# A hybrid SSD and attention step: norm weight by broadcast, first gate product ahead, y's banks emptied first, scan entry behind a piece

## The chip, the cores and the metric

The kernel runs on one core of a Trainium2 chip. The metric is the device time of one execution in microseconds (us). The engines are TensorE (PE in the profile; PEld is its weight load), VectorE (DVE), ScalarE (ACT), GpSimd (POOL) and SyncE (SP), which here issues the DMAs. Each engine works through its own instructions in order and waits on semaphores for the others.

## What is computed

Two layers on a residual stream of 1,024 prompt tokens and 64 sample tokens (8 requests of 8 tokens) with 1,024 features: a Mamba-2 SSD layer, then a latent-attention layer, then a last norm. All is float32 to the outside. This change concerns the SSD layer alone:

```python
u    = rms_norm(h, norm_w)                       # x * rsqrt(mean x^2 + eps) * norm_w
proj = u @ w_in                                  # z (2048) | x, B, C (4096) | dt (32)
xbc  = silu(causal_conv(xbc, w, b))              # four taps
y    = ssd_scan(xs, softplus(dt + dt_bias), -exp(a_log), B, C, state)   # chunks of 128
y    = (y + d_skip * xs) * silu(z)
y    = y * rsqrt(mean over each of 8 groups of 256 of y^2 + eps) * ssd_norm_w
h    = h + y @ w_out
```

In a chunk, cb = C B^T is masked and multiplied by a decay matrix M; that times x*dt gives the part within the chunk (py), x*dt faded to the chunk's end times B gives the state's gain (st), and C times the state before gives the rest of y.

## The kernel before

**Precision.** A float32 operand is split into a rounded high part and the rest (xh and xl, woh and wol, yha and yla): ACT casts the high part, DVE subtracts it. A product is three matmuls (high*high, high*low, low*high). Line 130 is any such cast, line 131 any such subtraction, lines 89 and 101 the matmuls.

**Order.** For the SSD layer the instructions of every engine stand in the order in which the program emits them, so moving a call in the code moves its instructions on every queue that it uses. Tokens go in 9 tiles (8 of 128, the last with the 64 sample tokens).

**PSUM banks** have tags: tr 2 (all transposes), pj 2 (projections), cb, y, pv and st one each. A tile that takes a bank waits until the last reader of the bank's previous tile is done.

**Start (`First.begin`, `First.norm`).** SP loads x of tile 0, the gate's weights (four quarters z0 to z3, two DMAs each), the norm's weight as one row, the bias of dt sent to all partitions (dtb), and further tiles of x. Four matmuls of a column of ones by the weight's row (two in the program, line 586, each two on the chip) spread it over the partitions into two banks; DVE copies them to the tile nw. Then for each tile: `square` (ACT, with the sum), `root` (DVE, then POOL's power), `scale` (DVE, line 616: x times root times nw, in place), `turn` (8 transposes, line 625), `take` (the split into xh and xl, ACT then DVE), `gate` (24 matmuls with z's weights into pz). The gate's weights are split by `split_z` on ACT and DVE. In between come two batches of small transposes: vecp (convolution weights and norm weights, in the bank of cb) and cvp (the sample's conv state, in the bank of y).

**Groups and scan entry.** Eight groups follow, each with projections of x, B, C and z in pieces (`proj(t)`), the convolution, the silu and a scan over the 9 tiles. Each group's scan runs beside the next group's projections, one step per tile. The first scan is entered at the end of `First`'s projection: front(0) is on TensorE the transposes trp and the product cb of chunk 0; then ACT's last silu; front1(0) reads trp and cb on ACT and DVE, DVE's last step there being cbm, the masked cb.

**Out-projection (`OutProj`, loop over t from 0).** Its first half, "a", runs beside the scan of the last group. Tile i of y is loaded, scaled (ACT, line 1121), transposed into the two tr banks (ytpa, line 1131) and split into yha and yla (lines 130, 131). Tile 0 is multiplied in four parts, in steps 1 to 4, while the weights still arrive: in each step two of the eight weight pieces are scaled and split (woh on ACT, line 1223; wol on DVE, line 1230). The later tiles take a step for each half (`proj`). `scan.ew(t)` is the scan's work off TensorE (M's exponential and product, the state S, y, xD), then front(t+1); `scan.pe(t)` is st and py. In a step the order was: the later tiles' product, scan.ew, the weights, oa.ew (store, split, scale, loads), scan.pe, a part of tile 0, evictions, and the next transposes. yla is the last reader of the tr banks, from which the scan's next transposes (trp, line 809) take theirs.

Of the kernel before, what the change touches and what calls it, by code (L numbers as in the profile page):

```python
# [9 lines left out]
F32 = mybir.dt.float32  # L10
F32R = mybir.dt.float32r
AF = mybir.ActivationFunctionType
# [5 lines left out]
D = 1024  # L18
# [3 lines left out]
T = SEQ + NB * NT  # L22
# [60 lines left out]
PB = dict(PB1)  # L83
# [90 lines left out]
def load_vectors(k, vp, psum):  # L174
# [9 lines left out]
    k.vec = cp.tile([128, 196], F32, name="vec")  # L184
    p = psum.tile([128, 512], F32, tag="cb", name="vecp", bufs=PB["cb"])
    nc.tensor.transpose(p[:, :128], r1, k.ident)
# [370 lines left out]
class First(Flow):  # L557
# [5 lines left out]
    def begin(self):  # L563
        k, nc, cp = self.k, self.k.nc, self.k.cp
        self.load_x(0)
        for q in range(4):
            self.load_z(q)
        row = self.rp.tile([128, RAW], F32, tag="raw", name="nrow", bufs=2)[0:1, :D]
        nc.sync.dma_start(row, k.I["norm_w"][0:1])
        nc.sync.dma_start(k.dtb, k.I["ssd_dt_bias"][0].partition_broadcast(128))  # L570
        for i in range(1, 4):
            self.load_x(i)
        ones = self.xp.tile([1, 128], F32, name="nones")
        nc.gpsimd.memset(ones, 1.0)
        self.ssq = cp.tile([128, 9], F32, name="ssq9")
        nc.gpsimd.memset(self.ssq, 1.0)
        self.rs = cp.tile([128, 9], F32, name="rs9")
        k.dtr = self.zd.tile([128, 9, H], F32, name="dtr")
        nc.gpsimd.memset(k.dtr[64:, 8], 0.0)
        self.square(0)  # L580
        self.root(0)
        self.nw = self.xp.tile([128, D], F32, name="nw")
        for hf in range(2):
            c = slice(512 * hf, 512 * hf + 512)
            p = self.psum.tile([128, 512], F32, tag=("y", "pv")[hf], name=f"nwp{hf}", bufs=1)
            nc.tensor.matmul(p, ones, row[:, c], start=True, stop=True)
            nc.vector.tensor_copy(self.nw[:, c], p)
        self.scale(0)
        self.turn(0)
# [28 lines left out]
    def turn(self, i):  # L618
        m, x = TILES[i][1], self.xt[i]
        self.p[i] = []  # L620
        for q in range(2):
            p = self.psum.tile([128, 512], F32, tag="tr", name=f"xtp{i}_{q}", bufs=PB["tr"])
            for a in range(4):
                d = 4 * q + a
                self.k.nc.tensor.transpose(p[:, a * 128 : a * 128 + m], x[:m, d * 128 : d * 128 + 128], self.k.ident[:m, :m])
            self.p[i].append(p)
# [27 lines left out]
    def norm(self, vectors, states):  # L654
        self.begin()
        self.split_z(0)
        self.split_z(1)
        self.take(0)
        self.split_z(2)
        self.split_z(3)  # L660
        for i in (1, 2):
            self.square(i)
            self.root(i)
        self.scale(1)
        self.turn(1)
        for n in range(1, 10):
            ev = self.gate(n - 1)
            if n < 9:
                self.take(n)
            if n + 2 < 9:  # L670
                self.square(n + 2)
                self.root(n + 2)
            if n + 1 < 9:
                self.scale(n + 1)
            if n + 3 < 9:
                self.load_x(n + 3)
            if n == 2:
                ssd_consts(self.k)
            if n in (2, 6):
                next(vectors)  # L680
            if n in (3, 7):
                next(states)
            if n in (5, 6):
                self.load(n - 5)
            if n in (8, 9):
                self.split(n - 8)
                self.load(n - 6)
            if n + 1 < 9:
                self.turn(n + 1)
            ev()  # L690
# [23 lines left out]
    def blocks(self, dt, nxt, scan_of):  # L714
# [43 lines left out]
        self.conv(3, slice(512, n))  # L758
        self.tails(3)
        scan.front(0)  # L760
        self.silu(1, slice(512, SEQ))
        scan.front1(0)
        return scan

# [333 lines left out]
class OutProj:  # L1098
# [85 lines left out]
    def ew(self, t):  # L1184
        for d, f in ((-1, self.split), (-3, self.scale), (-1, self.load_x), (-5, self.load_y)):
            for i, T in enumerate(self.start):
                if t == T + d and not (i == 0 and self.tag == "a" and d < 0):
                    f(i)
        for i, T in enumerate(self.start):
            if t == T + (4 if i == 0 else 2):  # L1190
                self.store(i)

    def pe(self, t):
# [50 lines left out]
def ssd_groups(k, first, scan, nxt, pools, sp, psum, st, left, right, als):  # L1244
    tc, nc = k.tc, k.nc
    pscan = None
    for g in range(1, G):
        fl, nxt = nxt, Flow(k, g + 1, pools) if g < G - 1 else None
        nscan = Scan(k, fl, (sp, psum))
        for t in range(21):  # L1250
            ev = fl.proj(t)
            fl.weights_in(t)
            if nxt and t == 20:
# [42 lines left out]
    for t in range(B0 + 22):  # L1296
        evs = oa.work(t) if t >= A0 + 4 else []
        if t < 22:
            scan.ew(t)
        if t == 0:  # L1300
            pscan.ew(21)
            oa.split(0)
            oa.load_x(0)
# [29 lines left out]
        if t == 22:  # L1333
            group_rstd(k, 4, 8)
        oa.ew(t)
        ob.ew(t)
# [7 lines left out]
        if t < 21:  # L1344
            scan.pe(t)
        if A0 <= t < A0 + 4:
            evs += oa.work(t)
        for ev in evs:
# [1143 lines left out]
```

## Time and profile before

| | |
|---|---|
| median of 3 runs | 1977.34 us (1976.92 to 1978.05) |
| profiled execution | 1978.51 us, its span 1976.7 us |
| mean granted TensorE clock | 0.985 |
| busy: TensorE, DVE, ACT, POOL | 1890.7, 1185.7, 1108.4, 835.6 us |
| DMA | 206.50 MB, 104 GB/s on the mean |

A row of a timeline has the start in us from the span's start, the time it took, the engine, the line, the operation with output and inputs, and how many it sums up; brackets hold the engine's idle time before it and what ended that. SPq is the issue of a DMA, not its transfer. In the waits view a row has what waited, for what, the us in total, the times and the longest. TensorE's matmuls overlap: their spacing is shorter than their duration.

### The profile page before, as it was taken

The numbers are of one execution on the slowest core, as the hardware profiler recorded it, in microseconds if no ns is written. First come the engines' busy times: TensorE is split into PE (matmuls) and PEld (weight loads), VectorE is DVE, ScalarE is ACT, GpSimd is POOL, SyncE is SP. The second block draws the span as 40 slices with busy tenths as digits, with TensorE's granted clock in tenths as the row PEclk, the third lists the DMA queues.
The fourth block names the chain that finished last, engine by engine and source line by source line (L and its number), as shares of the span: only waits on it lengthen the run. The fifth ranks groups of instructions, "written<-read, shape, count | busy, mean of one in ns | idle before, by whom it ended". The sixth has DMA issues, their size and how long they took to land.

```text
span 1976.7 us, 33806 instructions
## 1 busy us (share of the span) xinstructions
PE 1890.7 (96%) x11957; PEld 1733.9 (88%) x11957; DVE 1185.7 (60%) x2564; ACT 1108.4 (56%) x2604; POOL 835.6 (42%) x1139
## 2 busy tenths in 40 slices
PE   6999999999999999799999999999999999789998
PEld 5999999999999999687687998898888887678887
DVE  5457575757575757545425315476787786666665
ACT  4556666666666666643324314335777777655552
POOL 2137373737373657233000001103565556866661
PEclk9999999999999999899999999999999999899999
DMA  4213332323333332544454432232221213554441
GB/s 140 53 55 90 89 95 84 96 84 95 90 91 92 89 90 85 194 158 155 169 184 141 140 146 82 67 109 68 53 67 40 53 42 97 158 162 143 147 149 38
DMA packets 182403, 206.50 MB, mean 104 GB/s; under 512 B 18989, under 2 KB 147897, under 8 KB 181850
## 3 DMA queue, kind: packets, MB, share of 16 engines
q1 hardware_dynamic: 177402, 185.33, 30.9%
q0 software_dynamic: 4752, 18.88, 2.9%
q8 instruction: 95, 1.56, 0.3%
q14 instruction: 74, 0.61, 0.1%
q10 hardware_dynamic: 80, 0.13, 0.0%
HBM read 150.98 MB, written 53.15 MB: 103 GB/s over the span
## 4 chain that ended last, share of the span: by engine, by line
PE 78%; POOL 7%; issue 4%; DVE 4%; DMA 4%; ACT 3%; SPq 0%; POOLq 0%; DVEq 0%; ACTq 0%
PE pj L89 24%; PE pj L101 9%; PE pq L101 6%; PE pob L101 4%; PE poa L101 4%; POOL kvl L2139 4%; PE py L865 3%; PE sc L1793 2%; PE st L1826 1%; PE o L1859 1%; PE st L1827 1%; PE pz L101 1%; PE st L1828 1%; PE o L1858 1%; PE o L1857 1%
## 5 line engine op out<-in xcount | busy, mean ns | idle before, releaser
L89 PE MATMUL pj<-xh,wih 128*128 128x384 f32 (+1 forms) x768 | 255.1, 332 | 0.0
L89 PE MATMUL pj<-xh,wil 128*128 128x384 f32 (+1 forms) x768 | 250.7, 326 | 0.0
L89 PE MATMUL pj<-xl,wih 128*128 128x384 f32 (+1 forms) x768 | 250.4, 326 | 0.0
L1840 POOL TENSOR_TENSOR tl<-P,th 128x384 fp32r<-128x384 f32 (+1 forms) x144 | 133.0, 929 | 134.0 <-ACT P L1838 74.5
L131 DVE TENSOR_TENSOR wil<-wraw,wih 128x512 fp32r<-128x512 f32 x92 | 70.4, 765 | 172.6 <-ACT wih L130 172.5
L902 POOL TENSOR_TENSOR y<-y,xD 128x256 f32<-128x256 f32 x64 | 84.0, 1313 | 151.4 <-DVE y L901 141.0
L89 PEld LDWEIGHTS pj<-xh,wih 128*128 128x128 f32 x768 | 144.5, 188 | 0.2
L89 PEld LDWEIGHTS pj<-xl,wih 128*128 128x128 f32 x768 | 144.4, 188 | 0.3
L89 PEld LDWEIGHTS pj<-xh,wil 128*128 128x128 f32 x768 | 144.1, 188 | 0.0
L101 PE MATMUL pj<-wih,xh 128*128 128x256 f32 x504 | 143.3, 288 | 0.0
L101 PE MATMUL pj<-wil,xh 128*128 128x256 f32 (+1 forms) x504 | 139.2, 282 | 0.0
L1837 ACT ACTIVATE th<-st 128x512 fp32r<-128x512 f32 x192 | 94.4, 492 | 68.6 <-PE st L1833 46.8
L497 DVE SCALAR_TENSOR_TENSOR acc<-raw,vec,acc 128x1112 f32<-128x1112 f32 x84 | 130.5, 1554 | 0.2
L101 PE MATMUL pj<-wih,xl 128*128 128x256 f32 x448 | 126.6, 283 | 0.0
L2139 POOL TENSOR_TENSOR kvl<-pgr,kvh 128x256 fp32r<-128x256 f32 x128 | 98.2, 794 | 52.4 <-ACT kvh L2137 52.4
L131 POOL TENSOR_TENSOR xddl<-xdd,xddh 128x256 fp32r<-128x256 f32 x64 | 64.0, 1000 | 110.1 <-ACT xddh L130 110.1
L130 ACT CAST Ch<-acc 128x128 fp32r<-128x128 f32 x56 | 16.9, 302 | 157.0 <-PE py L89 157.0
L101 PEld LDWEIGHTS pj<-wih,xh 128*128 128x128 f32 x504 | 96.0, 191 | 0.0
L1838 ACT ACTIVATE P<-st 128x512 f32<-128x512 f32 x192 | 93.4, 486 | 2.7 <-DVE tl L1840 2.0
L101 PEld LDWEIGHTS pj<-wil,xh 128*128 128x128 f32 (+1 forms) x504 | 93.0, 185 | 0.6
L840 ACT ACTIVATE M<-M,tok 128x128 f32<-128x128 f32 (+1 forms) x288 | 90.6, 388 | 1.8 <-DMA M<-acs_d 1.8
L101 PEld LDWEIGHTS pj<-wih,xl 128*128 128x128 f32 x448 | 85.4, 191 | 0.0
(984 smaller groups left out, 6276.7 us busy)
## 6 DMA issues: line engine op xcount, KB each, us to landing
wraw<-in_ssd_w_in SPq DMA_DIRECT2D x92, 256.0 KB
M<-acs_d SPq DMA_DIRECT2D x64, 256.0 KB
y_d<-xD SPq DMA_DIRECT2D x64, 128.0 KB
s<-in_state_ssm SPq DMA_DIRECT2D x32, 256.0 KB
out_s_ssm<-s SPq DMA_DIRECT2D x32, 256.0 KB
wraw<-in_ssd_w_out SPq DMA_DIRECT2D x16, 512.0 KB
q_d<-qt SPq DMA_DIRECT2D x32, 192.0 KB
qp<-q_d SPq DMA_DIRECT2D x8, 768.0 KB
```

The costliest lines, as they stand in the source:

```text
L89: nc.tensor.matmul(out, a, b, start=(i == 0), stop=(i == n - 1))
L101: nc.tensor.matmul(o, a, b, start=(j == 0), stop=(j == len(ops) - 1))
L131: (eng or nc.vector).tensor_tensor(lo, src, hi.bitcast(F32), op=ALU.subtract)
L497: nc.vector.scalar_tensor_tensor(acc, self.raw[bi][:, j : j + n], k.convw[j][:, blk : blk + 1], acc, op0=ALU.mult, op1=ALU.add)
L840: nc.scalar.activation(M[:m, h, :m], M[:m, h, :m], AF.Relu, bias=c.tk[:, 0, 4 * g + h : 4 * g + h + 1], scale=-1.0)
L865: nc.tensor.matmul(py[:m, h * 64 : h * 64 + 64], c.M[:m, h, :m], c.xdt[:m, h * 64 : h * 64 + 64], start=True, stop=True)
L902: nc.gpsimd.tensor_tensor(y[:m], y[:m], c.xD[:m], op=ALU.add)
L1793: nc.tensor.matmul(ps[:, :n], qh[:96, 128 * i : 128 * i + 128], kh[:96, 512 * c : 512 * c + n], start=True, stop=True)
L1837: nc.scalar.activation(th[:, :n], ps[:, :n], AF.Exp, scale=SCALE)
L1838: nc.scalar.activation(P[:, :n], ps[:, :n], AF.Exp, scale=SCALE)
L1840: eng.tensor_tensor(tl[:, :n], P[:, :n], th[:, :n].bitcast(F32), op=ALU.subtract)
L2139: nc.gpsimd.tensor_tensor(rl[:, r], raw[:, r], rh[:, r].bitcast(F32), op=ALU.subtract)
```

## The change

It does four things.

1. **Norm weight.** The row, the ones, the matmuls and the copies go; SP loads the weight into all 128 partitions by one DMA (512 KB), right behind x0. The order of the loads behind it is z0, z1, x1, z2, z3, dtb, x2, x3, x4. An activation of a 128x9 tile without use stands ahead of the first square on ACT.
2. **First tiles.** TensorE's order becomes turn(0), gate(0), turn(1), turn(2), gate(1), turn(3) and so on; odd tiles turn in the banks of cb and st. The square of tile 1 goes ahead of the splits of z2 and z3. Tiles are scaled and turned one step earlier than their gate asked for before. vecp uses the bank of y.
3. **Scan entry.** front(0), the silu and front1(0) are emitted behind proj(0) of the next group.
4. **Out-projection.** The split of y ("cast") goes ahead of the scan's work in each step, and the parts of tile 0 are emitted ahead of scan.pe.

On TensorE at the start, before (nwp is the spread weight, xtp the transposes of a tile, pz the gate's product):

```order
L586 MATMUL nwp_142<-nrow,nones 128x512
L586 MATMUL nwp_145<-nrow,nones 128x512
L625 MATMUL xtp_0_149<-ident,xt_107 128x128 x4
L625 MATMUL xtp_1_154<-ident,xt_107 128x128 x4
L625 MATMUL xtp_0_188<-ident,xt_124 128x128 x4
L625 MATMUL xtp_1_193<-ident,xt_124 128x128 x4
L101 MATMUL pz_199<-zdh_159,xh 128x288
L101 MATMUL pz_199<-zdl_160,xh 128x288
```

and with the change, first

```order
L622 MATMUL xtp_0_143<-ident,xt_107 128x128 x4
L622 MATMUL xtp_1_148<-ident,xt_107 128x128 x4
L101 MATMUL pz_183<-zdh_153,xh 128x288
L101 MATMUL pz_183<-zdl_154,xh 128x288
L101 MATMUL pz_183<-zdh_153,xl 128x288
```

and behind the gate's 24 matmuls

```order
L101 MATMUL pz_183<-zdl_174,xh 128x288
L101 MATMUL pz_183<-zdh_173,xl 128x288
L622 MATMUL xtp_0_208<-ident,xt_117 128x128 x4
L622 MATMUL xtp_1_213<-ident,xt_117 128x128 x4
L622 MATMUL xtp_0_227<-ident,xt_126 128x128 x4
L622 MATMUL xtp_1_232<-ident,xt_126 128x128 x4
L101 MATMUL pz_241<-zdh_153,xh 128x288
```

The spreading is gone, and the second tile's transposes stand behind the first gate's product, with those of the third tile directly behind them.

On TensorE at the scan entry, before (pj_11 is the first group's last piece, pj_0 the next group's first):

```order
L89 MATMUL pj_11_1088<-xh,wil 128x320
L809 MATMUL trp_0_1125<-ident,acc_1012 128x128
L810 MATMUL trp_0_1125<-ident,acc_1012 128x128
L812 MATMUL trp_0_1125<-ident,acc_760 128x128
L814 MATMUL cb_0_1129<-acc_760 128x128
L89 MATMUL pj_0_1149<-xh,wih 128x384
```

and with the change

```order
L89 MATMUL pj_0_1117<-xh,wil 128x384
L809 MATMUL trp_0_1144<-ident,acc_1004 128x128
L810 MATMUL trp_0_1144<-ident,acc_1004 128x128
L812 MATMUL trp_0_1144<-ident,acc_752 128x128
L814 MATMUL cb_0_1148<-acc_752 128x128
L809 MATMUL trp_1_1183<-ident,acc_1004 128x128
L810 MATMUL trp_1_1183<-ident,acc_1004 128x128
L812 MATMUL trp_1_1183<-ident,acc_752 128x128
L814 MATMUL cb_1_1187<-acc_752 128x128
L89 MATMUL pj_1_1189<-xh,wih 128x384
```

The transposes and cb of chunk 0 have moved behind pj_0, directly ahead of those of chunk 1, which stood there before too.

On ACT in the third step of the out-projection, before (y_0 is the scan's first output, M its decay matrix, xddh the faded input's high part, Sh the state's):

```order
L910 ACTIVATE y_0_10765,yssq<-xD_0_10715 128x256
L1223 ACTIVATE woh_10826<-wraw,vec 128x1024
L1223 ACTIVATE woh_10829<-wraw,vec 128x1024
L846 ACTIVATE M_2_10752<-M_2_10752 128x512
L130 CAST xddh_2_10872<-xdd_2_10809 128x256
L130 CAST Sh_1_10877<-S_2_10799 128x256
L130 CAST yha_10887<-ytpa_10858 128x512
L130 CAST yha_10887<-ytpa_10863 128x512
L1121 ACTIVATE yta_10779<-yta_10779,yssq 128x256 x4
```

and with the change

```order
L910 ACTIVATE y_0_10769,yssq<-xD_0_10721 128x256
L1228 ACTIVATE woh_10830<-wraw,vec 128x1024
L1228 ACTIVATE woh_10833<-wraw,vec 128x1024
L130 CAST yha_10872<-ytpa_10850 128x512
L130 CAST yha_10872<-ytpa_10855 128x512
L846 ACTIVATE M_2_10756<-M_2_10756 128x512
L130 CAST xddh_2_10882<-xdd_2_10813 128x256
L130 CAST Sh_1_10887<-S_2_10803 128x256
L1121 ACTIVATE yta_10783<-yta_10783,yssq 128x256 x4
```

The two casts of y have moved from behind the scan's M, xddh and Sh to ahead of them; DVE's yla moves likewise.

On TensorE in the first step of the out-projection with a part, before (poa is tile 0's product):

```order
L809 MATMUL trp_1_10688<-ident,acc_9836 128x128
L810 MATMUL trp_1_10688<-ident,acc_9836 128x128
L812 MATMUL trp_1_10688<-ident,acc_9429 128x128
L814 MATMUL cb_1_10692<-acc_9429 128x128
L89 MATMUL st_0_10729<-xddh_0_10654,BTh_0_10607 128x256
L89 MATMUL st_0_10729<-xddl_0_10655,BTh_0_10607 128x256
L89 MATMUL st_0_10729<-xddh_0_10654,BTl_0_10608 128x256
L865 MATMUL py_0_10730<-xdt_0_10610,M_0_10446 128x64 x4
L1156 MATMUL poa_10738<-woh_10674,yha_10666 128x512
```

and with the change

```order
L809 MATMUL trp_1_10680<-ident,acc_9828 128x128
L810 MATMUL trp_1_10680<-ident,acc_9828 128x128
L812 MATMUL trp_1_10680<-ident,acc_9421 128x128
L814 MATMUL cb_1_10684<-acc_9421 128x128
L1156 MATMUL poa_10686<-woh_10666,yha_10642 128x512
```

The part's first matmul now follows cb_1 directly; its twelve matmuls stand ahead of st_0 and py_0.

The diff:

```diff
--- before.py
+++ after.py
@@ -182,7 +182,7 @@
     nc.sync.dma_start(r2[64:68], I["mla_q_norm_w"].rearrange("o (b c) -> (o b) c", c=128))
     yield
     k.vec = cp.tile([128, 196], F32, name="vec")
-    p = psum.tile([128, 512], F32, tag="cb", name="vecp", bufs=PB["cb"])
+    p = psum.tile([128, 512], F32, tag="y", name="vecp", bufs=PB["y"])
     nc.tensor.transpose(p[:, :128], r1, k.ident)
     nc.tensor.transpose(p[:, 128:196], r2, k.ident[:68, :68])
     nc.vector.tensor_copy(k.vec, p[:, :196])
@@ -563,28 +563,24 @@
     def begin(self):
         k, nc, cp = self.k, self.k.nc, self.k.cp
         self.load_x(0)
-        for q in range(4):
-            self.load_z(q)
-        row = self.rp.tile([128, RAW], F32, tag="raw", name="nrow", bufs=2)[0:1, :D]
-        nc.sync.dma_start(row, k.I["norm_w"][0:1])
+        self.nw = self.xp.tile([128, D], F32, name="nw")
+        nc.sync.dma_start(self.nw, k.I["norm_w"][0].partition_broadcast(128))
+        self.load_z(0)
+        self.load_z(1)
+        self.load_x(1)
+        self.load_z(2)
+        self.load_z(3)
         nc.sync.dma_start(k.dtb, k.I["ssd_dt_bias"][0].partition_broadcast(128))
-        for i in range(1, 4):
+        for i in (2, 3, 4):
             self.load_x(i)
-        ones = self.xp.tile([1, 128], F32, name="nones")
-        nc.gpsimd.memset(ones, 1.0)
         self.ssq = cp.tile([128, 9], F32, name="ssq9")
         nc.gpsimd.memset(self.ssq, 1.0)
         self.rs = cp.tile([128, 9], F32, name="rs9")
         k.dtr = self.zd.tile([128, 9, H], F32, name="dtr")
         nc.gpsimd.memset(k.dtr[64:, 8], 0.0)
+        nc.scalar.activation(self.rs, self.ssq, AF.Square)
         self.square(0)
         self.root(0)
-        self.nw = self.xp.tile([128, D], F32, name="nw")
-        for hf in range(2):
-            c = slice(512 * hf, 512 * hf + 512)
-            p = self.psum.tile([128, 512], F32, tag=("y", "pv")[hf], name=f"nwp{hf}", bufs=1)
-            nc.tensor.matmul(p, ones, row[:, c], start=True, stop=True)
-            nc.vector.tensor_copy(self.nw[:, c], p)
         self.scale(0)
         self.turn(0)
 
@@ -619,7 +615,8 @@
         m, x = TILES[i][1], self.xt[i]
         self.p[i] = []
         for q in range(2):
-            p = self.psum.tile([128, 512], F32, tag="tr", name=f"xtp{i}_{q}", bufs=PB["tr"])
+            tag = ("cb", "st")[q] if i % 2 else "tr"
+            p = self.psum.tile([128, 512], F32, tag=tag, name=f"xtp{i}_{q}", bufs=PB[tag])
             for a in range(4):
                 d = 4 * q + a
                 self.k.nc.tensor.transpose(p[:, a * 128 : a * 128 + m], x[:m, d * 128 : d * 128 + 128], self.k.ident[:m, :m])
@@ -656,37 +653,38 @@
         self.split_z(0)
         self.split_z(1)
         self.take(0)
+        self.square(1)
+        self.root(1)
         self.split_z(2)
         self.split_z(3)
-        for i in (1, 2):
-            self.square(i)
-            self.root(i)
         self.scale(1)
-        self.turn(1)
-        for n in range(1, 10):
-            ev = self.gate(n - 1)
-            if n < 9:
-                self.take(n)
+        self.square(2)
+        self.root(2)
+        for n in range(9):
+            ev = self.gate(n)
+            if n == 0:
+                self.turn(1)
+            if n < 8:
+                self.take(n + 1)
+            if n + 3 < 9:
+                self.square(n + 3)
+                self.root(n + 3)
             if n + 2 < 9:
-                self.square(n + 2)
-                self.root(n + 2)
-            if n + 1 < 9:
-                self.scale(n + 1)
-            if n + 3 < 9:
-                self.load_x(n + 3)
-            if n == 2:
+                self.scale(n + 2)
+                self.turn(n + 2)
+            if n + 5 < 9:
+                self.load_x(n + 5)
+            if n == 1:
                 ssd_consts(self.k)
+            if n in (1, 6):
+                next(vectors)
             if n in (2, 6):
-                next(vectors)
-            if n in (3, 7):
                 next(states)
-            if n in (5, 6):
+            if n in (4, 5):
+                self.load(n - 4)
+            if n in (7, 8):
+                self.split(n - 7)
                 self.load(n - 5)
-            if n in (8, 9):
-                self.split(n - 8)
-                self.load(n - 6)
-            if n + 1 < 9:
-                self.turn(n + 1)
             ev()
 
     def conv(self, bi, c):
@@ -757,10 +755,12 @@
         self.conv0(3, slice(512, n))
         self.conv(3, slice(512, n))
         self.tails(3)
+        return scan
+
+    def enter(self, scan):
         scan.front(0)
         self.silu(1, slice(512, SEQ))
         scan.front1(0)
-        return scan
 
     def state_out(self, t, scan):
         k, nc = self.k, self.k.nc
@@ -1182,13 +1182,18 @@
         k.nc.sync.dma_start(k.h_d[t0 : t0 + m], self.xr[i][:m])
 
     def ew(self, t):
-        for d, f in ((-1, self.split), (-3, self.scale), (-1, self.load_x), (-5, self.load_y)):
+        for d, f in ((-3, self.scale), (-1, self.load_x), (-5, self.load_y)):
             for i, T in enumerate(self.start):
-                if t == T + d and not (i == 0 and self.tag == "a" and d < 0):
+                if t == T + d and not (i == 0 and self.tag == "a"):
                     f(i)
         for i, T in enumerate(self.start):
             if t == T + (4 if i == 0 else 2):
                 self.store(i)
+
+    def cast(self, t):
+        for i, T in enumerate(self.start):
+            if t == T - 1 and i in range(self.tag == "a", 9):
+                self.split(i)
 
     def pe(self, t):
         for i, T in enumerate(self.start):
@@ -1249,6 +1254,8 @@
         nscan = Scan(k, fl, (sp, psum))
         for t in range(21):
             ev = fl.proj(t)
+            if g == 1 and t == 0:
+                first.enter(scan)
             fl.weights_in(t)
             if nxt and t == 20:
                 nxt.split(1)
@@ -1294,12 +1301,14 @@
     oa.yp = st.enter_context(open_pool(tc, name="ya", bufs=1))
     ob = OutProj(k, oa.yp, [], psum, NWA, h_loader(k), "b", B0)
     for t in range(B0 + 22):
-        evs = oa.work(t) if t >= A0 + 4 else []
+        evs = oa.work(t)
+        if t == 0:
+            oa.split(0)
+        oa.cast(t)
         if t < 22:
             scan.ew(t)
         if t == 0:
             pscan.ew(21)
-            oa.split(0)
             oa.load_x(0)
         if t < 4:
             oa.ws += wo.split(wa, 2 * t, 2 * t + 1)
@@ -1332,6 +1341,7 @@
             group_rstd(k, 4, t // 2 - 2)
         if t == 22:
             group_rstd(k, 4, 8)
+        ob.cast(t)
         oa.ew(t)
         ob.ew(t)
         if t == B0 + 13:
@@ -1343,8 +1353,6 @@
             evs += ob.work(t)
         if t < 21:
             scan.pe(t)
-        if A0 <= t < A0 + 4:
-            evs += oa.work(t)
         for ev in evs:
             ev()
         oa.pe(t)
```

## The prediction

> **What bounds the kernel now.** I read the page's busy shares first, then the waits of TensorE, which add up every stall with what ended it.
>
> ```profile
> PE 1890.7 (96%) x11957; PEld 1733.9 (88%) x11957; DVE 1185.7 (60%) x2564; ACT 1108.4 (56%) x2604; POOL 835.6 (42%) x1139
> PE trp L809 <- DVE yla L131: 16.5, 4, 6.8
> PE nwp L586 <- DMA nrow<-in_norm_w: 9.3, 1, 9.3
> PE xtp L625 <- DVE xt L616: 7.6, 2, 5.4
> PE cb L814 <- DVE cbm L833: 1.4, 1, 1.4
> PE trp L809 <- ACT acc L710: 1.4, 1, 1.4
> ```
>
> TensorE is busy for 1890.7 of 1976.7 us, so a gain can only come from its 86 idle us or from time at a lower clock. The last five rows (waited for, us in total, times, longest) are the stalls that this change touches: 9.3 + 7.6 at the start, 16.5 at the banks of y's transposes, 1.4 + 1.4 at the scan entry, together 36.2 us. That is the ceiling. The sum depends on what stands behind each wait, so I read the timeline of each place.
>
> **The start.**
>
> ```profile
> 4.93 1.28 ACT L608 ACT_TABLE_LOAD   x1 [4.93 <-DMA xt<-in_x_prompt]
> 6.17 0.37 SPq L570 DMA_DIRECT2D dtb<-in_ssd_dt_bias  x1
> 6.22 1.06 ACT L608 ACTIVATE sq<-xt 128x1024 f32<-128x1024 f32 x1
> 7.71 0.56 POOL L204 TENSOR_TENSOR rs<-rs,nhalf 128x1 f32<-128x1 f32 x1 [6.51 <-DVE rs L199]
> 9.26 3.75 PE L586 MATMUL nwp<-nrow,nones 1*128 1x512 f32 x4 [9.26 <-DMA nrow<-in_norm_w]
> 13.84 1.28 DVE L616 SCALAR_TENSOR_TENSOR xt<-xt,rs,nw 128x1024 f32<-128x1024 f32 x1
> 15.18 1.97 PE L625 MATMUL xtp<-ident,xt 128*128 128x128 f32 x8 [2.17 <-DVE xt L616]
> 16.33 0.59 ACT L130 CAST xh<-xtp 128x512 fp32r<-128x512 f32 x1 [7.83 <-PE xtp L625]
> 17.67 1.25 ACT L130 CAST zdh<-zraw 128x576 fp32r<-128x576 f32 x2
> 18.41 1.42 DVE L131 TENSOR_TENSOR zdl<-zraw,zdh 128x576 fp32r<-128x576 f32 x2
> 28.26 1.04 PE L625 MATMUL xtp<-ident,xt 128*128 128x128 f32 x8
> 28.26:54.00 25.74, 25.45 (x197) 24.58 (x196) 17.15 (x30) 13.92 (x28) 7.77 (x6) 1.00 0.15 33
> ```
>
> The last row is the windows view (stretch, its length, then busy us of PE, PEld, DVE, ACT and POOL, granted clock, DMA share and GB/s). From the third tile's transposes at 28.26 on, TensorE is full. So the start is worth what it moves that instruction. Eight transposes take 1.97 us at 15.18 and 1.04 there: TensorE ran at half speed before.
>
> Now: x0 lands at 4.93, but the table load comes after it. The dummy activation puts the load ahead, so the square runs 4.93 to 6.0, and the root ends near 7.0 (before, POOL's power ended 1.0 us behind the square's 7.28). The weight now comes as 512 KB instead of 4 KB plus four matmuls (3.75) and two copies. No row of before is this load. The nearest is the decay load M, also one DRAM row sent to all partitions:
>
> ```profile
> 121.79 0.44 SPq L795 DMA_DIRECT2D M<-acs_d  x1
> 125.52 0.69 ACT L840 ACTIVATE M<-M,tok 128x128 f32<-128x128 f32 x2 [1.19 <-DMA M<-acs_d]
> GB/s 0 0 54 160 252 295 339 305 319 345 318 276 76 35 53 64 291 379 410 410 429 422 416 429 416 313 90 41 13 11 15 49 67 57 54 139 391 385 252 233
> ```
>
> M's 256 KB took at most 3.73 us from issue to use; twice that from an issue near 1.6 lands at 9.1, the upper bound. The lower bound is the rate of the strip (40 slices of 0.65 us up to 26): 512 KB at about 320 GB/s, 1.6 us behind x0's landing, 6.5. I take 7.0, since a queue that is already streaming pays M's fixed part only once. Then scale(0) runs 7.05 to 8.3, turn(0) 8.4 to 10.4, xh and xl until 11.7; sq(1) is moved ahead of the last two z splits (11.0 to 12.2; x1, some 2.2 MB into the queue, is there by about 9), the z casts (1.25) follow to 13.4, and scale(1) stands behind their low halves (to 14.2) on DVE, 14.3 to 15.5. The first gate product fills TensorE from 10.2, waiting at the end for the last low half. turn(1) runs from 15.6, xh(1) and sq(3) to 18.9, then root, scale(2) 19.1 to 20.4, turn(2) at 20.5 instead of 28.26: **7.7 us** earlier.
>
> Taken off: slices 12 to 15 of the strip (76, 35, 53 and 64 GB/s, 7.8 to 10.4 us) are the bias load dtb, 16 KB in small pieces, with x1 behind it. x1 is now moved past it, x2 and x3 still stand behind it; 0.4 us for that, between 0 and 3. TensorE idles from about 17 to 20.5, so it may again start at half speed; 1.7 us (one clock window, priced below), between 0 and 3.4. The weight vectors' transpose goes to the bank of y, where the conv state's transposes follow in the same bank and wait for DVE's copy:
>
> ```profile
> 50.01 0.36 DVE L188 COPY vec<-vecp 128x196 f32<-128x196 f32 x1 [0.29 <-PE vecp L187]
> ```
>
> That is 0.36 us plus two hand-overs, 0.6. **Start: 7.7 − 0.4 − 1.7 − 0.6 = +5.0**, from 0.7 to 7.1.
>
> **The scan entry.**
>
> ```profile
> 113.08 0.33 PE L809 MATMUL trp<-ident,acc 128*128 128x128 f32 x1 [1.43 <-ACT acc L710]
> 117.06 1.06 ACT L710 ACTIVATE acc<-acc 128x1024 f32<-128x1024 f32 x1 [2.67 <-DVE acc L696]
> 119.46 0.28 DVE L833 TENSOR_TENSOR cbm<-cb,masku 128x128 f32<-128x128 f32 x1
> 119.79 0.49 PE L814 MATMUL cb<-acc 128*128 128x128 f32 x2 [1.44 <-DVE cbm L833]
> 111.42:114.83 3.41, 1.99 (x14) 1.75 (x13) 0.93 (x2) 2.32 (x4) 0.33 (x2) 1.00 0.00 1
> 892.99:896.42 3.43, 1.07 (x8) 0.74 (x7) 3.34 (x7) 3.21 (x8) 3.02 (x4) 1.00 0.98 334
> 896.42:899.83 3.41, 3.41 (x12) 2.82 (x11) 2.13 (x6) 1.03 (x3) 1.76 (x3) 0.50 0.85 280
> ```
>
> The next group's first piece moves ahead of the chunk's transposes, which takes the first stall away. But the second, at 119.79, is set by ACT's silu at 117.06 and DVE behind it, whose order is unchanged. TensorE reaches it earlier and waits longer: 1.43 + 1.44 become one gap of 2.9. No gain, and a risk: windows with 1.99 of 3.41 us busy kept the clock at 1.00, while one with 1.07 busy (the 2.36 us gap below) was followed by a window at 0.50, which costs half of 3.41, **1.7 us**. A gap of 2.9 leaves some window under half busy unless a window's edge halves it; I take three quarters of the price, **−1.3**, between 0 and −1.7.
>
> The Trainium skill (TensorE: Matmul & The Clock Gate, Part 1) says that the clock falls after an idle window of about 3.4 us and advises against gaps above about 3 us; by it the merged gap would cost nothing and the sum would be 1.3 better. The 0.50 behind a gap of 2.36 disagrees, so the sum goes by the row.
>
> **The first steps of the out-projection.**
>
> ```profile
> 808.41 0.47 PE L809 MATMUL trp<-ident,acc 128*128 128x128 f32 x1 [6.75 <-DVE yla L131]
> 809.20 2.48 DVE L1230 SCALAR_TENSOR_TENSOR wol<-wraw,vec,woh 128x1024 fp32r<-128x1024 f32 x2 [0.25 <-ACT woh L1223]
> 818.56 2.58 DVE L1230 SCALAR_TENSOR_TENSOR wol<-wraw,vec,woh 128x1024 fp32r<-128x1024 f32 x2 [1.20 <-ACT woh L1223]
> 825.16 2.48 DVE L1230 SCALAR_TENSOR_TENSOR wol<-wraw,vec,woh 128x1024 fp32r<-128x1024 f32 x2 [2.28 <-ACT woh L1223]
> 831.06 0.47 PE L809 MATMUL trp<-ident,acc 128*128 128x128 f32 x1 [6.53 <-DVE yla L131]
> 834.99 0.69 DVE L1175 TENSOR_TENSOR xra<-xra,poa 128x512 f32<-128x512 f32 x1 [3.38 <-PE poa L1156]
> 836.25 0.39 PE L101 MATMUL poa<-woh,yha 128*128 128x512 f32 x1
> ```
>
> Here the largest stalls stand, 6.75 and 6.53. The first cast now leaves ahead of the scan's work, so the transposes of 808.41 can start near 804. But the four weight pieces (rows wol) are still split two per step behind the same ACT and DVE work, and each part of tile 0, now ahead of the scan's products, waits for them: wol 0 and 1 end at 811.7 whatever TensorE does. So part 0 ends near 815.2, the scan's st/py behind it near 817.2, part 1 near 820.2; part 2 waits for wol5 (818.56 + 2.58 = 821.1) and ends at 823.5, st/py at 825.1 instead of 820.8. Behind that ACT's cast of Ch (one buffer, free when py has read it) goes later, and with it the last two weight pieces: 828.1 to 830.7 instead of 825.16 to 827.64. y's cast then follows them at once and ends at 832. The first eviction follows DVE's scan work near 834.7, and the whole product of tile 1 starts near 835.4 instead of 836.25. **+0.5** of the 0.85, between −3 (two half-speed windows more) and +6 (half of the stalls go).
>
> **The later steps.**
>
> ```profile
> 878.65 0.33 PE L809 MATMUL trp<-ident,acc 128*128 128x128 f32 x1 [0.86 <-DVE yla L131]
> 894.93 1.27 DVE L131 TENSOR_TENSOR yla<-ytpa,yha 128x512 fp32r<-128x512 f32 x2
> 895.67 0.33 PE L809 MATMUL trp<-ident,acc 128*128 128x128 f32 x1 [2.36 <-DVE yla L131]
> 908.46 0.63 PE L1131 MATMUL ytpa<-ident,yta 128*128 128x128 f32 x4 [1.60 <-ACT xddh L130]
> ```
>
> Nothing but the order on ACT and DVE delays yla there; with y's casts first both stalls go, 0.86 + 2.36, and the half-speed window behind the second, 1.7. M's product and the scan's state come later by the casts' time, which the matmuls of the tile's product cover; without that cover each such step would lose the 1.27 us of yla. At 908.46 the transposes' second half now takes a bank that the cast of the first must free, about 1.9 instead of 1.60: −0.3. **+4.6**, from 2.5 to 4.9. All stages behind are unchanged and shift along.
>
> **Sum:** 5.0 − 1.3 + 0.5 + 4.6 = 8.8 us off the profiled execution's 1978.51, 1969.7; that execution stands 1.2 above the median of 1977.34, so **1968.5** in the median.
>
> **Rivals.** *The stalls really go:* no window is lost at the start (+7.1) or the entry (0), the first steps give half of their stalls (+6), and the later steps 4.6: 17.7, about 1959.6. The size of the 16.5 us row speaks for it, the rows of wol against it. *Gains eaten:* start at its low end (+0.7), entry −1.7, first steps −3, later steps 4.6: +0.6, about 1976.7. For it: each new gap can call up a half-speed window, and DMA-bound tiles at the start. *Slower:* the broadcast load moves at dtb's rate. 16 KB in about 2.6 us is 6.3 GB/s, and 512 KB would take 83 us; scale(0) would run near 85 instead of 13.84, less the 3.8 of the other terms: about 2045. It loses as soon as the weight lands after some 17.6 us (13.84 plus those 3.8). M's row, 256 KB in at most 3.73 us, speaks against it. *The change does not do what it says* is in the forecast already for the entry: the wait there is only merged.
>
> **How the numbers follow.** The forecast 0.57 (its own range 1964 to 1972.5, the terms' nearer bounds), the stalls go 0.18, eaten 0.20, slower 0.05. The range 1960.5 to 1976 reaches into the second and third cases. 0.2%, about what can be told from no change, is 4 us: faster is all of the first two and a quarter of the third, 0.80; same 0.14; slower 0.06, the fourth and the worst edge of the third.
>
> **What would show it.** Right: nw landed by 7 to 9, third tile's transposes near 20 to 22; one gap near 2.9 ahead of the entry's second cb; in the first steps matmuls of poa that wait for wol instead of trp for yla; no trp of later steps that waits for yla. Wrong: the table load not ahead of x0, transposes past 25, an entry without a gap, or the product of tile 1 over 3 us from where it was.

## The result, and the profile after

The changed kernel takes 1968.19 us in the median of 5 runs (1965.63 to 1970.02); the kernel before, on the same chip, 1978.05 (1976.92 to 1980.03). The ratio is 0.9948, with a 95% interval of 0.9933 to 0.9962: 10.3 us faster, between 7.5 and 13.3. The forecast was 8.8 us and 1968.5. The profiled execution has a span of 1966.8 us, 9.9 less than before.

TensorE's waits after the change (what waited, for what, us in total, times, longest):

```profile
PE xtp L622 <- DVE xt L612: 8.5, 1, 8.5
PE poa L1156 <- ACT woh L1228: 6.3, 2, 4.3
PE xtp L622 <- DVE dtr L646: 3.4, 1, 3.4
PE cb L814 <- DVE cbm L833: 3.1, 1, 3.1
PE trp L809 <- DVE yla L131: 2.2, 1, 2.2
PE ytpa L1131 <- DVE yla L131: 1.8, 1, 1.8
PE poa L1156 <- DVE wol L1235: 1.4, 2, 0.8
PE ytpa L1131 <- DVE yha L131: 0.9, 1, 0.9
PE cvp L314 <- DVE vec L188: 0.5, 1, 0.5
```

The row of 16.5 us (trp for yla) is down to 2.2, but more than half of what it lost stands in new rows: the parts of tile 0 wait 6.3 + 1.4 us for the split weights, which they had not shown before. At the scan entry 1.4 + 1.4 has become 3.1. The sums of the waits fell less than the old rows suggest.

Where the time went shows in how far ahead of the kernel before the same instruction stands. The starts are rows of the two timelines:

| place | before | after | ahead | gained since |
|---|---|---|---|---|
| third tile's transposes | 28.26 | 19.99 | 8.27 | 8.27 |
| fourth tile's transposes | 32.56 | 26.79 | 5.77 | −2.50 |
| second cb at the scan entry | 119.79 | 114.83 | 4.96 | −0.81 |
| first transposes of y | 800.02 | 796.63 | 3.39 | −1.57 |
| first whole product (tile 1) | 836.25 | 830.47 | 5.78 | +2.39 |
| tile 6's transposes of y | 906.23 | 895.10 | 11.13 | +5.35 |
| first transposes of half "b" | 948.6 | 938.6 | 10.0 | −1.1 |
| end of the span | 1976.7 | 1966.8 | 9.9 | −0.1 |

The start's own timeline after the change:

```profile
2.01 0.21 ACT L581 ACTIVATE rs<-ssq 128x9 f32<-128x9 f32 x1
5.05 1.06 ACT L604 ACTIVATE sq<-xt 128x1024 f32<-128x1024 f32 x1 [2.83 <-DMA xt<-in_x_prompt]
6.62 0.56 POOL L204 TENSOR_TENSOR rs<-rs,nhalf 128x1 f32<-128x1 f32 x1 [5.54 <-DVE rs L199]
7.21 1.28 DVE L612 SCALAR_TENSOR_TENSOR xt<-xt,rs,nw 128x1024 f32<-128x1024 f32 x1 [0.74 <-POOL rs L204]
8.54 1.97 PE L622 MATMUL xtp<-ident,xt 128*128 128x128 f32 x8 [8.54 <-DVE xt L612]
15.29 1.06 ACT L604 ACTIVATE sq<-xt 128x1024 f32<-128x1024 f32 x1 [1.97 <-DMA xt<-in_x_prompt]
19.99 1.94 PE L622 MATMUL xtp<-ident,xt 128*128 128x128 f32 x8 [3.43 <-DVE dtr L646]
26.79 1.04 PE L622 MATMUL xtp<-ident,xt 128*128 128x128 f32 x8
```

The first scale waits for POOL's root and not for a DMA, so the broadcast weight was there by 7.2: the slow-broadcast rival is out. The third tile's transposes take 1.94 us, half speed, and the fourth tile's come 6.80 behind them instead of the 4.30 of before: 2.50 of the 8.27 us are paid back there. The windows view (columns as in the prediction) shows the granted clock at half in between:

```profile
20.00:23.00 3.00, 3.00 (x14) 3.00 (x15) 1.11 (x2) 1.62 (x3) 0.24 (x1) 0.50 0.14 32
23.00:26.00 3.00, 3.00 (x15) 3.00 (x15) 1.64 (x3) 0.60 (x2) 1.64 (x2) 0.51 0.59 199
```

The out-projection's first steps after the change:

```profile
800.45 0.33 PE L809 MATMUL trp<-ident,acc 128*128 128x128 f32 x1 [2.19 <-DVE yla L131]
805.82 0.80 PE L1156 MATMUL poa<-woh,yha 128*128 128x512 f32 x1 [4.28 <-ACT woh L1228]
807.14 0.80 PE L1156 MATMUL poa<-wol,yha 128*128 128x512 f32 x1 [0.53 <-DVE wol L1235]
823.87 0.49 PE L1156 MATMUL poa<-woh,yha 128*128 128x512 f32 x1 [2.01 <-ACT woh L1228]
825.19 0.80 PE L1156 MATMUL poa<-wol,yha 128*128 128x512 f32 x1 [0.82 <-DVE wol L1235]
830.47 0.47 PE L101 MATMUL poa<-woh,yha 128*128 128x512 f32 x1 [0.62 <-DVE xra L1175]
```

The transposes wait 2.19 us instead of 6.75, and the second stall of 6.53 is gone; but TensorE then waits 4.28 and 2.01 for woh, and 0.53 and 0.82 for wol. So of the 13.3 us (6.75 and 6.53) 11.1 went and 7.6 came back in another place, and the stretch gained only 2.4.

### The profile page after: what moved, and what is told of

It reads as the page before. It is cut to its first block, busy times and chain, and to the rows that moved or that the text cites. A ratio compares the mean times of both kernels' runs of the same rounds, so it can differ in the third digit from the quotient of the medians.

```text
span 1966.8 us, 33784 instructions
## 1 busy us (share of the span) xinstructions
PE 1890.8 (96%) x11953; PEld 1735.2 (88%) x11953; DVE 1185.9 (60%) x2562; ACT 1108.1 (56%) x2605; POOL 833.7 (42%) x1138
## 4 chain that ended last, share of the span: by engine, by line
PE 77%; POOL 7%; issue 4%; DMA 4%; DVE 4%; ACT 3%; SPq 1%; POOLq 0%; DVEq 0%; ACTq 0%
PE pj L89 23%; PE pj L101 9%; PE pq L101 6%; PE pob L101 4%; PE poa L101 4%; POOL kvl L2147 3%; PE py L865 3%; PE sc L1801 2%; PE st L1834 2%; PE st L1835 2%; PE st L1836 2%; PE o L1867 2%; PE o L1866 1%; PE o L1865 1%; PE pk L101 1%
```

## Experiments

Each kernel was compared with runs of the kernel before on the same chip. All intervals are 95%, and gains in us are worked out from the ratios. A statement about a place in the kernel rests on one profiled execution of each kernel.

### The parts alone: e1 to e4

> The kernel before with the start of the change alone (weight by broadcast load, tables first, first gate product ahead, vecp in the bank of y). Theory: the start is worth what it moved in the changed kernel, third tile's transposes near 20.0, then about 5.8 us ahead of before once one half-speed window has been paid, 5.0 to 5.8 behind the wait for vec's copy; in all 5.0 to 5.8 us faster, and nothing else moves. Rival: an earlier start only shifts the wait to the scan entry (its chain runs on ACT and DVE), then under 3 us of it arrive behind the entry.

```diff
-        for q in range(4):
-            self.load_z(q)
-        row = ...
+        nc.sync.dma_start(self.nw, k.I["norm_w"][0].partition_broadcast(128))
+        self.load_z(0)
...
```

(begin, turn, norm and vecp's bank as in the change, the rest as before.) Measured: 1971.01 us, ratio 0.9972 (0.9961 to 0.9984), 5.5 us faster. The profiled execution shows the third tile at 20.47 (7.79 ahead), the fourth at 24.80 (7.76 ahead), and 6.8 to 6.9 from the entry to the end of the groups: the whole gain arrives there, so the rival falls. Here the transposes ran at full speed, with no window lost:

```profile
20.47 1.06 PE L622 MATMUL xtp<-ident,xt 128*128 128x128 f32 x8 [3.26 <-DVE dtr L646]
24.80 1.06 PE L622 MATMUL xtp<-ident,xt 128*128 128x128 f32 x8
```

> The kernel before with the scan entry behind the next group's first piece alone. Theory: the two stalls of 1.43 and 1.44 us become one of about 2.9 to 3.1 that ends with the same masked product; 0 to 0.2 us lost, or 1.5 to 1.9 us where a half-speed window follows the gap. Rival: the piece covers the first stall, 1.4 us faster.

```diff
-        scan.front(0)
-        self.silu(1, slice(512, SEQ))
-        scan.front1(0)
         return scan
+
+    def enter(self, scan):
+        scan.front(0)
+        self.silu(1, slice(512, SEQ))
+        scan.front1(0)
...
             ev = fl.proj(t)
+            if g == 1 and t == 0:
+                first.enter(scan)
```

Measured: 1979.29 us, ratio 1.0008 (0.9998 to 1.0018): 1.6 us slower, between 0.4 faster and 3.6 slower. Its profile has one gap where there were two, and the full clock behind it (windows view again):

```profile
120.55 0.49 PE L816 MATMUL cb<-acc 128*128 128x128 f32 x2 [3.06 <-DVE cbm L835]
120.00:123.00 3.00, 2.45 (x15) 2.45 (x16) 1.19 (x4) 2.97 (x6) 0.17 (x1) 1.00 0.00 0
```

That cb is 0.76 us behind the kernel before, all of it present at the third tile already, ahead of the edit; across the entry nothing changes. In the changed kernel the same gap is followed by half speed:

```profile
114.83 0.79 PE L814 MATMUL cb<-acc 128*128 128x128 f32 x2 [3.07 <-DVE cbm L833]
116.00:117.00 1.00, 1.00 (x4) 1.00 (x4) 0.32 (x1) 0.99 (x2) 0.00 (x0) 0.50 0.00 0
```

So the gap is merged, not filled, and costs 0 or 1.6 us depending on whether a half-speed window follows. The rival, 1.4 us gained, is refuted.

> The kernel before with y's casts ahead of the scan's work in each step of the out-projection alone, tile 0's parts left behind the scan's products. Theory: this order carries nearly all that the out-projection gained, about 2 us in the first steps and about 5.4 less 0.9 behind them: 6 to 7 us faster. Rival: the first steps gain only with the parts ahead too: about 4.5 us faster.

```diff
-        for d, f in ((-1, self.split), (-3, self.scale), (-1, self.load_x), (-5, self.load_y)):
+        for d, f in ((-3, self.scale), (-1, self.load_x), (-5, self.load_y)):
...
+        if t == 0:
+            oa.split(0)
+        oa.cast(t)
         if t < 22:
             scan.ew(t)
...
+        ob.cast(t)
         oa.ew(t)
```

Measured: 1972.12 us, ratio 0.9967 (0.9955 to 0.9980), 6.5 us faster. In its profile the first steps gain 3.2 us, the later ones 5.5, and 2.3 are lost again by the end of half "b".

> The kernel before with tile 0's parts ahead of the scan's products alone, y's casts left behind the scan's work. Theory: no more than 1.5 us either way, since the parts wait for the split weights and the later casts keep their place; the later stalls of 0.86 and 2.36 us remain. Rival: 2 to 2.5 us faster, the whole gain of the first steps.

```diff
-        evs = oa.work(t) if t >= A0 + 4 else []
+        evs = oa.work(t)
...
-        if A0 <= t < A0 + 4:
-            evs += oa.work(t)
```

Measured: 1975.37 us, ratio 0.9989 (0.9979 to 0.9998), 2.2 us faster, between 0.4 and 4.2; the first steps are 1.8 us shorter in the profile. That is a little over what the theory allowed (1.5) and near the rival; the interval holds both. The first stall stays, the second has become the wait for the weights:

```profile
808.47 0.47 PE L809 MATMUL trp<-ident,acc 128*128 128x128 f32 x1 [6.75 <-DVE yla L131]
827.35 0.50 PE L1156 MATMUL poa<-woh,yha 128*128 128x512 f32 x1 [2.01 <-ACT woh L1223]
```

The four gains add up to 5.5 − 1.6 + 6.5 + 2.2 = 12.6 us against 10.3 for the whole, which is within the intervals. The profiles show an overlap all the same: in the first steps casts and parts alone gain 3.2 and 1.8, together 2.4. The next run takes them apart.

> The changed kernel with tile 0's parts put back behind the scan's products (y's casts stay first). Theory: beside the casts the parts' place is worth nothing, since each step waits for the split weights anyway; tile 1's product starts 0 to 1 us earlier than in the changed kernel. Rival: the parts add what they gave alone, so 1.5 to 2.2 us slower than the changed kernel.

```diff
-        evs = oa.work(t)
+        evs = oa.work(t) if t >= A0 + 4 else []
...
         if t < 21:
             scan.pe(t)
+        if A0 <= t < A0 + 4:
+            evs += oa.work(t)
```

Measured: 1969.74 us, ratio 0.9958 (0.9942 to 0.9973). From y's first transposes to tile 1's product the kernels take, by their timelines:

| kernel | start of ytpa | start of the product | us between |
|---|---|---|---|
| before | 800.02 | 836.25 | 36.23 |
| parts alone | 800.08 | 834.54 | 34.46 |
| changed | 796.63 | 830.47 | 33.84 |
| casts alone | 799.34 | 832.34 | 33.00 |
| changed without parts ahead | 797.99 | 830.88 | 32.89 |

With the casts first, the parts ahead cost 0.95 us rather than gain. Four other kernels that leave these steps as in the change (e5, e7, e8, e11) took 33.8 to 34.4 us there, so the two with the casts first and the parts behind, at 32.9 and 33.0, do stand apart. The times speak less clearly: by the ratios this kernel is 2.0 us slower than the changed one, as the rival had it, but the intervals overlap. Its profiled execution lost 1.4 at the start, ahead of the edit: the fourth tile's transposes come at 28.22 instead of 26.79.

### The entry back: e5

> The changed kernel with the scan entry put back ahead of the next group's first piece. Theory: the merged gap of 3.07 us splits into two of about 1.4, no half-speed window follows it, and everything behind is 1.5 to 1.7 us earlier than in the changed kernel where that had such a window, the same where not; 0 to 1.7 us faster than the changed kernel. Rival: the moved piece was worth its first stall, 1.4 us slower.

(The entry's hunks of e2 undone in the changed kernel.) Measured: 1967.32 us, ratio 0.9955 (0.9941 to 0.9969). The gap splits again into 1.43 and 1.45, and the clock stays full. The row is from its windows:

```profile
114.00:117.00 3.00, 3.00 (x19) 3.00 (x19) 1.35 (x2) 2.97 (x6) 0.31 (x1) 1.00 0.20 47
```

In the profile it is 1.23 us ahead of the changed kernel before the entry (the start's clock) and 2.72 behind it: 1.5 at the entry, as the theory has it for an execution with a half-speed window. The times cannot tell the two kernels apart.

### What the entry and the first steps wait for: e6, e7

> The changed kernel with the first group's second cb in the bank pv, which is free there, so that it does not wait for the first cb's reader. Theory: the gap of 3.07 us at the entry goes, and the next wait is for M (ACT's relu and exponential behind a table load) ahead of the first st and py: 1.5 to 3 us faster than the changed kernel. Rival: the whole gap moves to that wait: 0 to 0.5.

```diff
-        pc = c.cb = self.bank("cb", "cb" + c.tag)
+        pc = c.cb = self.bank("pv" if self.g == 0 and i == 1 else "cb", "cb" + c.tag)
```

Measured: 1967.66 us, ratio 0.9953 (0.9936 to 0.9969). The gap at cb is gone, and a new wait stands behind the next piece, ahead of the scan's first product (0.6 us more follow there for the low part of xdd on POOL):

```profile
PE st L89 <- ACT xddh L130: 1.7, 1, 1.7
```

From ahead of the entry to behind it this execution gains 0.34 us on the changed kernel, with a stretch at half speed behind the gap in both. So the bank was what cb waited for, but what bounds the place is ACT's chain of the scan (silu, M, xddh): the rival, the wait moves, holds. This is also why moving a piece on TensorE could not gain there.

> The changed kernel with the split of the out-projection's weights ahead of the scan's work in steps 0 to 3 (behind y's cast). Theory: what bounds the first steps is the weights' split behind the scan on ACT and DVE, so the waits of the parts for woh (4.28 and 2.01 us) and wol (0.53 and 0.82) go, and tile 1's product starts 3 to 6 us earlier than in the changed kernel. Rival: M and the state come 2.2 us later in each step, and the scan's products wait in the parts' place: within 1 us of the changed kernel.

```diff
         oa.cast(t)
+        if t < 4:
+            oa.ws += wo.split(wa, 2 * t, 2 * t + 1)
+            wo.low()
+            if t < 2:
+                wo.load(2 * t + 4, 2 * t + 5)
         if t < 22:
             scan.ew(t)
...
-        if t < 4:
-            oa.ws += ...
```

Measured: 1966.28 us, ratio 0.9945 (0.9929 to 0.9962). The waits for woh are gone and those for wol fall to 1.0 us in three, so the weights' split behind the scan was what the parts waited for. But a new stall appears:

```profile
PE ytpa L1131 <- DVE BTl L829: 3.5, 1, 3.5
PE poa L1156 <- DVE wol L1235: 1.0, 3, 0.5
```

With the fourth step's weights ahead of front1 on ACT and DVE, the transposes of chunk 2 stay in their bank 2 us longer, and y's second transposes wait for that bank. The steps take 31.87 us (795.49 to 827.36) against 33.84. Tile 1's product starts 3.1 us earlier, which reaches the 3 to 6 expected only because 1.1 of it was there ahead of the steps: the edit gained 2, since one wait took another's place.

### The start: e8, e11

> The changed kernel without the extra activation, so that ACT's table load again follows x0's landing. Theory: the first transposes come 1.1 to 1.3 us later, but the third tile's hang on x2 (its square waits for the DMA at 15.3) and come within 0.4 us of the changed kernel's; 0 to 0.4 us slower. Rival: the whole start shifts, 1.1 to 1.3 us slower to the end.

```diff
-        nc.scalar.activation(self.rs, self.ssq, AF.Square)
```

Measured: 1968.48 us, ratio 0.9960 (0.9946 to 0.9974). The first transposes come at 9.36 instead of 8.54, the third tile's at 20.88 instead of 19.99, 0.89 later; I had expected at most 0.4, so x2's landing did not hide it: the delay runs on over the second tile, whose transposes come at 16.58 instead of 15.46 and hold ACT's casts and DVE's next scale back. Yet the fourth tile's come at 25.21, 1.58 earlier than in the changed kernel, since no half-speed window fell there. In this execution the clock outweighs the term. By the ratios the kernel is 2.4 us slower than the changed one, but the intervals overlap, so what the extra activation is worth in time stays open.

> The changed kernel with dtb behind x2 in the queue, and tile 2's scale ahead of tile 1's split on DVE. Theory: the idle 3.43 us ahead of the third tile's transposes are x2's late landing and then DVE's order; x2 lands 2 to 2.5 us earlier, the third tile's transposes start near 17, and the kernel is 2 to 4 us faster. Rival: the chain goes on to tile 1's split on ACT, and the gate product of tile 1 waits instead: 0 to 1 us.

```diff
-        nc.sync.dma_start(k.dtb, ...)
-        for i in (2, 3, 4):
+        self.load_x(2)
+        nc.sync.dma_start(k.dtb, ...)
+        for i in (3, 4):
             self.load_x(i)
...
             if n == 0:
                 self.turn(1)
+                self.scale(2)
...
-                self.scale(n + 2)
+                if n:
+                    self.scale(n + 2)
```

Measured: 1965.13 us, ratio 0.9940 (0.9925 to 0.9955). The square of tile 2 runs at 13.93 instead of 15.29, and the idle 3.43 us shrink to 0.39:

```profile
13.93 1.06 ACT L605 ACTIVATE sq<-xt 128x1024 f32<-128x1024 f32 x1 [0.54 <-DMA xt<-in_x_prompt]
16.19 1.28 DVE L613 SCALAR_TENSOR_TENSOR xt<-xt,rs,nw 128x1024 f32<-128x1024 f32 x1 [0.65 <-POOL rs L204]
17.62 1.06 PE L623 MATMUL xtp<-ident,xt 128*128 128x128 f32 x8 [0.39 <-DVE xt L613]
22.78 1.06 PE L623 MATMUL xtp<-ident,xt 128*128 128x128 f32 x8 [0.89 <-DVE dtr L647]
```

The third tile stands 2.37 us ahead of the changed kernel, the fourth 4.0, 3.9 to 4.0 remain at every place read up to half "b", and 3.7 at the end of the span. The times show less, 1.6 us by the ratios with overlapping intervals. The theory holds in the profile: x2 behind dtb and DVE's order held the third tile. The two edits were made together; by the rows 1.4 of the 2.4 us is x2's landing (the square at 13.93 instead of 15.29) and the rest DVE's order. TensorE does not idle long here and keeps its full clock.

### Together: e10, e12

> The changed kernel with the weights' split ahead of the scan's work in steps 0 to 2 alone (step 3 as in the changed kernel) and the scan entry put back. Theory: the new stall of 3.55 us that all four steps showed, second transposes of y waiting behind the third step's weights, does not arise, the first part's wait stays away, the entry gives 0 to 1.7: tile 1's product 3 to 5 us earlier than in the changed kernel, and 3 to 6 us faster at the end. Rival: part 3's waits of 2.01 and 0.82 return in full with a half-speed window: 1.5 to 2.5 us faster only.

```diff
         oa.cast(t)
+        if t < 3:
+            oa.ws += wo.split(wa, 2 * t, 2 * t + 1)
...
-        if t < 4:
+        if t == 3:
             oa.ws += wo.split(wa, 2 * t, 2 * t + 1)
```

(And the entry's hunks undone.) Measured: 1963.70 us, ratio 0.9929 (0.9913 to 0.9944), 14.0 us faster than before; that is 3.8 more than the change, with overlapping intervals. The steps take 31.58 us (793.86 to 825.44). The stall of 3.55 is 0.53, part 3's waits of 1.50 and 0.82 remain. Tile 1's product is 5.0 us ahead of the changed kernel, 2.3 of it from these steps, the rest from the entry and from the start's clock.

> The two edits above together: start order, weights ahead in steps 0 to 2, entry put back. Theory: places far apart add up, 5 to 9 us faster than the changed kernel, 1959 to 1963. Rival: less than 4 us, where the clock's windows take back at one place what the other gives.

Measured: 1961.26 us in 5 runs (1959.88 to 1962.13), ratio 0.9918 (0.9904 to 0.9931): 16.2 us faster than the kernel before. Its interval lies wholly below the changed kernel's (0.9933 to 0.9962), so it beats both. Its rows show where:

```profile
18.13 1.06 PE L623 MATMUL xtp<-ident,xt 128*128 128x128 f32 x8 [1.00 <-DVE xt L613]
815.88 0.50 PE L1157 MATMUL poa<-woh,yha 128*128 128x512 f32 x1 [1.49 <-ACT woh L1229]
PE cb L815 <- DVE cbm L834: 1.5, 1, 1.5
```

The gain over the changed kernel, about 6 us by the ratios, is in the expected band of 5 to 9.

## Why the prediction was right

**The start: forecast +5.0, found 8.27 − 2.50 − 0.81 = 4.96.** The chain came out as worked: the first transposes at 8.54 (forecast 8.4), the third tile's at 19.99 (20.5). The weight was in time, as M's row had suggested. The wait behind vec's copy was 0.5 (0.6 forecast); the other 0.3 of the 0.81 was not traced. The term for the clock was sized at one window, 1.7, and was 2.5: the granted clock stands at 0.50 from about 19.1 to 25.9, the length of two windows. In the execution of the start alone it was 0. So the mechanism was right, but that the sum came out within 0.1 is luck: the third tile stood 1.0 further ahead than the 7.7 − 0.4 of the forecast, and the clock took 0.8 more. The 0.4 for x2 was too small in what it named: e11 shows that x2 behind dtb, together with DVE's order, held back 2.4 us directly, and 4 with the clock, that the change left lying. The ceiling of 36.2 us, counted from waits alone, left out that the spreading matmuls (3.75 us of TensorE) went too.

**The scan entry: forecast −1.3, found −1.57.** The wait was merged into one of 3.07 us (2.9 forecast) and in this execution a half-speed window followed. e2 shows the other outcome, 0, and taking the entry back (e5) gives 1.5. Three quarters of a window's price, as the forecast had it, was about right: from the second cb to the first st, six profiled executions with the merged gap took 4.5 us (e2) or 5.9 to 6.1 (the other five), and the seven with two gaps 4.5. By the idle window of about 3.4 us on the page of the Trainium skill that the prediction weighed (TensorE: Matmul & The Clock Gate, Part 1) the gap would have cost nothing; the row at 0.50 behind a gap of 3.07 disagrees, the 1.00 behind 3.06 in e2 agrees.

**The first steps: forecast +0.5, found +2.39; this is the term that was mis-sized.** The mechanism is the one described: the transposes no longer wait long, the parts wait for the split weights, and Ch's single buffer puts the last two weights late. The sign to look for named wol on DVE, but the larger waits are for woh on ACT, 6.3 us against 1.4. The size was off by 1.9 us, of which 0.35 had been taken off the forecast's own timeline (0.85) without a row for it. Moved back by the 3.39 us that it was ahead, the first part ended at 814.9 (forecast 815.2), the second at 818.9 (820.2), the third at 822.6 (823.5), the last low weights began at 827.2 (828.1), and tile 1's product at 833.9 (835.4). Some 0.8 us of it is the clock: st and py behind the first part took 1.17 us at full speed, where I had worked with 2.0, nearer to the 2.35 that they took at half speed before (809.39 to 811.74). The rest lies in DVE's work ahead of the first eviction, which came at 833.0 and not at 834.7; there M's product took 0.68 us instead of the 1.21 of before. And the parts' own place, on which I spent most of the working, cost 0.95 beside the casts (e9).

**The later steps: forecast +4.6, found +5.35 − 1.1 = 4.3.** Both stalls went, with the half-speed window. The new wait for the first half's cast was 1.8, as forecast at 1.9. The second new wait was missed: the sample tile's transposes wait 0.9 us for its cast, a row that stood in none of my steps.

**The rivals.** That the big stalls would really go is refuted by the 6.3 us that now wait for woh. That the gains would be eaten was right for single places (the entry, the fourth tile) and wrong for the sum.

## What to carry to other kernels

A stall in the waits view names the last releaser; before it is priced, ask what the waiting engine needs next. Here 13.3 us of waits for y's casts hid a chain of weight splits behind them: taking 11.1 of them away gave 2.4 us, while moving the splits ahead gave 2 more. A gap that is merged instead of filled can cost more than the two it replaced: half speed followed the merged gap of 3.1 us in five executions of six, and the gaps of 1.4 in none of seven.

## What the runs showed of the hardware that was not expected

The same instructions with the same gap ran at different clocks in different executions. Between the third and the fourth tile's transposes, with the same idle time of about 3.3 us ahead, the start of the change alone took 4.33 us, and the changed kernel without parts ahead 6.85:

```profile
21.37 1.94 PE L622 MATMUL xtp<-ident,xt 128*128 128x128 f32 x8 [3.26 <-DVE dtr L646]
28.22 1.03 PE L622 MATMUL xtp<-ident,xt 128*128 128x128 f32 x8
```

Five more executions of this start lay at 4.33 (e8), 5.4 (e7) and 5.6 to 5.7 (e5, e6 and e10). Likewise the gap of 3.06 to 3.07 at the scan entry was followed by half speed in the changed kernel and by full speed in e2. Where the edge of a clock window falls relative to the gap would explain this; no run here set it, so that cause is only argued. It may also be part of why the runs of one kernel spread by several us, which no run here shows. Landmarks of one profile must therefore be read with the granted clock beside them.
